# Attention rows stored as two half-precision planes and turned by transposing loads, with the stages of an output tile further apart

## The chip, the cores and the metric

The kernel runs on one core of one Trainium2 chip. A core has a matrix engine (TensorE, PE in the profile; its weight loads are listed apart as PEld), a vector engine (VectorE, DVE), an activation engine (ScalarE, ACT), a general engine (GpSimd, POOL) and an engine that mainly issues transfers (SyncE, SP). Each engine works through its own queue in the order in which the program fills it, and waits for the others through semaphores. Sixteen DMA engines move data between the chip's memory (DRAM), and the on-chip buffer (SBUF). PE writes its results to banks of a second on-chip memory (PSUM).

The metric is the device time of one execution in microseconds (us), as the median of several runs.

## What is computed

One decoder layer over 2048 positions of width 1024. The input `x` is normalised, scaled and shifted, and one projection makes everything that the two attention branches need. Branch A has 8 heads of width 64 with full causal attention and a forget-gate bias. Branch B has 8 query heads over 2 key/value heads, rotary positions, a window of 128 and a sink per head. Each branch output is multiplied by a SiLU gate; the two are joined and go through one output projection, a second normalisation and a gated residual sum.

```
h  = rms_norm(x, g_pre) * (1 + scale) + shift
qa, ka, va, fa, za, qb, kb, vb, zb = split(h @ w_in)
oa = forgetting_attention(qa, ka, va, fa + b_fgate) * silu(za)
ob = sliding_window_sink_attention(rope(qb), rope(kb), vb, sinks) * silu(zb)
y  = concat([oa, ob]) @ w_out
x + gate * rms_norm(y, g_post)
```

All inputs and the output are float32. The kernel keeps float32 accuracy on a half-precision matrix engine by writing each operand as a high plane (the value rounded to float16) and a low plane (the rest, in float16), and by summing three products: high by high, high by low, low by high.

## The kernel before

A program order is written out by hand. A list `late` holds work that is due some ticks later: `after(n, f)` runs `f` at the n-th following `tick()` (lines 185 to 195). Whatever `f` issues is then placed in the engines' queues at that point. Four stages follow each other.

1. Prologue (to about 166 us): the modulation, normalisation and turning of `x` into `hT`, and the first projections.
2. Windowed attention (about 166 to 396 us): 32 windows, one per pair of heads and pair of 128-row blocks (class `Pair`, lines 849 to 941, loop at lines 1122 to 1143). A window has four ticks. After the first tick come `maxima` (four DVE operations of line 881, and the sink columns copied by POOL at line 879); then units of projection work are filled in on PE; after the second tick `pv` of the window two earlier (PE, line 930); after the third tick `exps` (ACT, line 892) and `split`; the fourth tick issues the high split (ACT, line 909) with a transposing transfer from SBUF to SBUF on SP (line 910), and the next window's first tick the low split (DVE, line 914) with a second one (line 915). `scores` of the next window (PE, line 867) close the window. The output of `pv` is scaled one tick after it, in `out_` (line 934): DVE multiplies it by the reciprocal sums into `on` (line 936, [128 x 256] float32), and POOL issues its store to `o_d` (line 938).
3. Full attention (about 400 to 985 us): 8 heads of 20 steps (class `Step`, lines 1312 to 1368, loop from line 1613). A step is `exp32` (ACT, line 1335), a tick, `low` of the step before (DVE, line 1346), half of the filled-in work, `high` (ACT, line 1343), the next `scores` (PE, lines 1330 and 1331), a tick, `pv` of the step two before (PE, lines 1356 to 1359), and the other half. The filled-in work is projections (`punits`) and row maxima (`munits`: PE line 1281, DVE lines 1284 and 1286). At the end of each 512-row block of a head, 32 times in all, `pv` scales its result into `on` (DVE, line 1365) and SP issues the store to `o_d` (line 1366). In the last head the weights of the output projection are loaded and split, and the first output tiles begin: `load_o` and `load_z` at steps 1 to 6, `turn(4)` of tiles 0 and 1 at steps 6 and 8, products from step 10 on.
4. Output (about 985 us to the end): 16 tiles of 128 rows (class `Out`, lines 1440 to 1558). For tile t, `load` fetches the gate factors `z` and the 128 rows of `o_d` (SP, lines 1461 and 1455). `turn(lag)` issues eight PE transposes of float32 [128 x 128] blocks into two PSUM banks (line 1467), one tick later the gating by DVE (line 1476, two halves), two ticks later the sum of squares by ACT (line 1479), `lag` ticks later a small PE product over the partitions and a scale (line 1483), then the high split (ACT, line 1489) and the low split (DVE, line 1490). `product(n, k)` is one unit of three matmuls of 512 columns (line 1503); a tile has two halves n of eight units k. One tick after a half is done, `evac` has ACT sum its squares (line 1511) and DVE multiply it by the gate factors (line 1519), and gives its bank back. `root` and `store` follow 4 and 7 ticks after the second half (lines 1539 and 1553). A tick comes every second unit.

The order of stage 4 is the list `ounits` (lines 1562 to 1570): the products of tiles 0 and 1 first in alternation, then tile after tile, with `turn` of tile t+1 behind the third unit of tile t, and the load of tile t+2 ahead of tile t. `ofill` (line 1574) takes the next units; in the last head's steps it takes the first 33.

Buffers concerned: `onp` (line 700) has two `on`; `opa` (line 1171) and `opo` (line 1398) have two each of `ona` and, in `opa`, of the gate tiles `tz`. The row buffer of a tile is a part of `Ts[0]`, in rotation over t % 2 (lines 1454 and 1460).

Of the kernel before, what the change touches and what calls it, by code (L numbers as in the profile page):

```python
# [10 lines left out]
F32 = mybir.dt.float32  # L11
# [7 lines left out]
P = 128  # L19
# [21 lines left out]
def hybrid_layer(  # L41
# [33 lines left out]
    o_d = [dram.tile([CH, D], F32, name=f"o_d{t}") for t in range(NCH)]  # L75
# [112 lines left out]
    def after(n, f):  # L188
        late.append([n, f])
# [510 lines left out]
    onp = swa_pool("onp", 2)  # L700
# [148 lines left out]
    class Pair:  # L849
# [73 lines left out]
        def pv(self):  # L923
# [10 lines left out]
            def out_():  # L934
                on = onp.tile([P, 2, P], F32, tag="on", name="on")
                V.tensor_tensor(on[:].rearrange("p e (h d) -> p (e h) d", h=2), po[:],
                                self.rinv[:].unsqueeze(2).broadcast_to([P, 4, 64]), op=ALU.mult)
                G.dma_start(o_d[i // 4][(i % 4) * P:(i % 4 + 2) * P, (4 + j) * P:(5 + j) * P]
                            .rearrange("(e p) c -> p e c", p=P), on[:])
# [231 lines left out]
    op_ = foxl.enter_context(tc.tile_pool(name="opa", bufs=2, reuse_waits="tile"))  # L1171
# [140 lines left out]
    class Step:  # L1312
# [35 lines left out]
        def pv(self):  # L1348
# [12 lines left out]
            if self.last:  # L1361
# [4 lines left out]
                SP.dma_start(o_d[self.ci][:, hd * 64:(hd + 1) * 64].rearrange("(u p) d -> p u d", p=P), on[:])  # L1366
# [26 lines left out]
    def open_out():  # L1393
# [4 lines left out]
        op_ = foxo.enter_context(tc.tile_pool(name="opo", bufs=2, reuse_waits="tile"))  # L1398
# [16 lines left out]
        oio["r"] = [spare[:, 2 * CH * n:2 * CH * (n + 1)].bitcast(F32) for n in range(6)]  # L1415
        oio["j"] = [spare[:, CH * a:CH * b].bitcast(BF16) for a, b in ((12, 14), (14, 15), (15, 16))]
# [23 lines left out]
    class Out:  # L1440


        def __init__(self, t):
            self.t = t
            self.last = t == NB - 1
            self.cuts = (0, CH, CH + 3 * P, D) if self.last else (0, CH, D)
# [5 lines left out]
        def load_o(self):  # L1452
            t = self.t
            self.o = Ts[0][:, t % 2, :].bitcast(F32)
            SP.dma_start(self.o, o_d[t // 4][(t % 4) * P:(t % 4 + 1) * P, :])
# [7 lines left out]
        def turn(self, lag):  # L1463

            px = [bk[bank()][:].rearrange("p (k n) -> p k n", k=4) for _ in range(2)]
            for k in range(KT):
                PE.transpose(px[k // 4][:, k % 4, :], self.o[:, k * P:(k + 1) * P], ident[:])  # L1467
# [4 lines left out]

            def gate():
                for h in range(2):
                    z = self.z[:, 4 * h:4 * h + 4, :]
                    V.tensor_tensor(z, px[h], z, op=ALU.mult)  # L1476
# [9 lines left out]
            after(1, gate)  # L1486
            after(2, squares_)
            after(lag, scale_)
            after(lag + 1, lambda: A.activation(hi, self.z, AF.Copy, scale=self.sc[:]))  # L1489
            after(lag + 2, lambda: V.scalar_tensor_tensor(lo, self.z, self.sc[:], hi, op0=ALU.mult, op1=ALU.subtract))  # L1490

        def product(self, n, k):
# [15 lines left out]
            def evac():  # L1508
                if n == 0:
                    self.y = oio["y"]()  # L1510
                A.activation(oio["j"][1 + n % 2][:, :cc.stop - cc.start], py, AF.Square, accum_out=self.ss[:, n:n + 1])
                if self.last:
# [49 lines left out]
    ounits, oloads = [], {}  # L1562
    for t, n in [(0, 0), (1, 0), (0, 1), (1, 1)] + [(t, n) for t in range(2, NB) for n in range(len(outs[t].cuts) - 1)]:
        if n == 0 and t + 2 < NB:
            oloads[len(ounits)] = t + 2
        for q in range(KT):
            ounits.append(lambda t=t, n=n, q=q: outs[t].product(n, q))
            nxt = 2 if (t, n) == (0, 1) else t + 1 if n == 0 and 2 <= t < NB - 1 else None
            if q == 2 and nxt:
                ounits.append(lambda nxt=nxt: outs[nxt].turn(4))  # L1570
    opos = [0]
    N_IN = 4 * KT + 1

    def ofill(n, each=None):
        for _ in range(n):
            if opos[0] in oloads:
                outs[oloads[opos[0]]].load()
            ounits[opos[0]]()
# [151 lines left out]
```

## Time and profile before

| | |
|---|---|
| median of 3 runs (lowest to highest) | 1155.76 us (1154.94 to 1155.79) |
| the profiled execution: its own time | 1155.56 us |
| the profiled execution: span from first to last instruction | 1153.9 us |
| mean granted clock of TensorE | 0.995 |
| busy: PE, DVE, ACT, POOL | 1113.2, 909.9, 679.0, 166.4 us |
| DMA: moved in all, mean rate | 136.36 MB, 118 GB/s |

The span leaves out 1.66 us of the profiled execution's own time. Times in the views are microseconds from the start of the span; mean durations of single instructions are nanoseconds. A busy share is an average over stages with different limits. The chain of waits is followed back from the last instruction to whatever released each step. In a timeline row the bracket at the end tells how long the engine had sat idle and what ended that. In the rows by windows, the columns are the stretch, its length, the busy time of PE, PEld, DVE, ACT and POOL with their instruction counts, the granted clock, the mean busy share of the DMA engines, and GB/s. Matmuls are pipelined and their ends are modelled, so that a PE that shows as busy can hide gaps below about 0.15 us.

### The profile page before, as it was taken

To read this page: it belongs to the slowest core of one execution; us is meant where nothing else is said; L and a number is where in the kernel's file an instruction comes from. 1 tells how busy PE (TensorE), PEld (TensorE's weight loads), DVE (VectorE), ACT (ScalarE), POOL (GpSimd) and SP (SyncE) were. 2 spreads that over 40 slices of the span, in tenths; PEclk is the share of its full clock that TensorE was granted. 3 is DMA by queue.
4 is the path that set the end of the run, shared out by engine and by line. 5 is a ranking of instruction groups with operands and counts; after the bars stand their busy time and mean duration, and the time that the engine had idled before them with its cause. 6 is when DMAs were issued, how large, how long until landed. Compare 5 with 4: busy or idle time off the path is not lost. (4 is left out here: it accounts for less than half of the span.)

```text
span 1153.9 us, 27043 instructions
## 1 busy us (share of the span) xinstructions
PE 1113.2 (96%) x10514; PEld 651.5 (56%) x10514; DVE 909.9 (79%) x2330; ACT 679.0 (59%) x1124; POOL 166.4 (14%) x302
## 2 busy tenths in 40 slices
PE   5899999999999999999999999999999989999997
PEld 1466657655579865555555555555555555455554
DVE  6776668879888477889888989878797886766666
ACT  4666446556666515766767667676776698233331
POOL 2011122234322101111111201101010010000000
PEclk9999999999999999999999999999999999999999
DMA  9646426587777423323233232313121264464642
GB/s 330 223 138 169 107 71 135 111 171 141 174 145 121 96 61 84 85 78 81 78 82 98 61 89 63 66 38 98 43 56 38 66 185 154 156 211 166 203 168 88
DMA packets 162452, 136.36 MB, mean 118 GB/s; under 512 B 95356, under 2 KB 139428, under 8 KB 162324
## 3 DMA queue, kind: packets, MB, share of 16 engines
q1 hardware_dynamic: 152388, 106.39, 35.3%
q0 software_dynamic: 9456, 27.72, 9.1%
q8 instruction: 82, 1.34, 0.5%
q10 hardware_dynamic: 480, 0.53, 0.2%
q14 instruction: 46, 0.38, 0.1%
HBM read 70.97 MB, written 25.18 MB: 83 GB/s over the span
## 5 line engine op out<-in xcount | busy, mean ns | idle before, releaser
L1335 ACT ACTIVATE p<-sta,lift,scl_qk 128x1024 f32<-128x1024 f32 (+2 forms) x160 | 172.0, 1075 | 94.6 <-PE sta L1331 88.7
L335 PE MATMUL bk<-hT,wh_qk 128*128 128x512 f16 x768 | 197.9, 378 | 0.6 <-DVE a_m L1284 0.6
L1503 PE MATMUL bk<-wohl,oz 128*128 128x512 f16 (+2 forms) x792 | 172.5, 372 | 2.2 <-DVE oz L1490 1.0
L1346 DVE TENSOR_TENSOR pha<-p,pha 128x1024 f16<-128x1024 f32 (+2 forms) x160 | 169.7, 1061 | 0.0
L1343 ACT ACTIVATE pha<-p 128x1024 f16<-128x1024 f32 (+2 forms) x160 | 148.1, 926 | 31.6 <-POOL p L1339 26.3
L1284 DVE TENSOR_REDUCE a_m<-bk 128x1 f32<-128x512 f32 x192 | 129.3, 683 | 36.3 <-PE bk L1281 35.4
L1503 PEld LDWEIGHTS <-oz 128*128 128x128 f16 x792 | 75.8, 99 | 83.2 <-issue 1.8
L1356 PE MATMUL poa<-vt,pha 128*128 128x65 f16 x1088 | 116.5, 193 | 1.6 <-DVE ona L1365 1.6
L1359 PE MATMUL poa<-vt,pha 128*128 128x65 f16 x1088 | 116.0, 192 | 1.3 <-DVE pha L1346 1.3
L1358 PE MATMUL poa<-vt,pha 128*128 128x64 f16 x1088 | 116.3, 194 | 0.0
L1330 PE MATMUL sta<-T 128*128 128x512 f16 (+1 forms) x320 | 109.6, 347 | 4.5 <-ACT p L1335 4.5
L1281 PE MATMUL bk<-T 66*128 66x512 f16 (+2 forms) x320 | 110.5, 348 | 2.2 <-DVE a_m L1284 2.2
L1356 PEld LDWEIGHTS <-pha 128*128 128x128 f16 x1088 | 101.6, 97 | 16.3 <-DVE ona L1365 2.9
L335 PEld LDWEIGHTS <-wh_qk 128*128 128x128 f16 x768 | 70.2, 97 | 71.6 <-issue 2.9
L1358 PEld LDWEIGHTS <-pha 128*128 128x128 f16 x1088 | 101.0, 97 | 13.4
L1331 PE MATMUL sta<-T 69*128 69x512 f16 (+1 forms) x320 | 108.0, 348 | 0.0
L1359 PEld LDWEIGHTS <-pha 128*128 128x128 f16 x1088 | 100.8, 99 | 1.6 <-DVE pha L1346 1.6
L335 PE MATMUL bk<-hT,wh_za 128*128 128x512 f16 x384 | 99.8, 378 | 0.0
L353 PE MATMUL bk<-wh_va,hT 128*128 128x128 f16 x1536 | 92.6, 219 | 0.0
L1339 POOL TENSOR_SCALAR_AFFINE_SELECT p<-p 128x256 f32<-128x256 f32 x64 | 31.9, 499 | 413.4 <-ACT p L1335 408.5
L335 PE MATMUL bk<-hT,wh_zb 128*128 128x512 f16 x384 | 90.8, 379 | 0.0
L353 PEld LDWEIGHTS <-hT 128*128 128x128 f16 x1536 | 87.5, 98 | 5.9 <-issue 3.5
(497 smaller groups left out, 1851.5 us busy)
## 6 DMA issues: line engine op xcount, KB each, us to landing
hT<-in_x_dram SPq DMA_DIRECT2D x20, 512.0 KB
wa<-in_w_ada_dram SPq DMA_DIRECT2D x16, 512.0 KB
T<-stq SPq DMA_DIRECT2D x128, 64.0 KB
T<-z_d SPq DMA_DIRECT2D x16, 512.0 KB
T<-o_d SPq DMA_DIRECT2D x16, 512.0 KB
z_d<-tz POOLq DMA_DIRECT2D x30, 256.0 KB, 2.9
out_dram<-hT SPq DMA_DIRECT2D x15, 512.0 KB
xt<-in_x_dram SPq DMA_DIRECT2D x12, 512.0 KB
```

Source lines behind the costliest of these rows:

```text
L335: PE.matmul(ps, whl[:, a, k, :], hT[ci][:, b, k, :], start=(k == 0 and n == 0), stop=(k == KT - 1 and n == 2))
L353: PE.matmul(ps[:, u * P:(u + 1) * P], hT[ci][:, a, k, u * P:(u + 1) * P], whl[:, b, k, :], start=(k == 0 and n == 0), stop=(k == KT - 1 an ...
L1281: PE.matmul(mx[:, :w], T[0:XM, 0, i * P:(i + 1) * P], T[0:XM, 2, pc * CH:pc * CH + w], start=True, stop=True)
L1284: V.tensor_reduce(m3[:, u, pc:pc + 1], mx[:, :w], axis=AX.X, op=ALU.max)
L1330: PE.matmul(self.st[:, o:o + w], T[:, 3, kb_], T[:, 1, qc], start=True, stop=False)
L1335: A.activation(self.p32[:, :self.w], self.st[:, :self.w], AF.Exp, scale=scl[f"qk{self.hd}"][:], bias=lift[:])
L1343: A.activation(self.ph[:, 0, :self.w], self.p32[:, :self.w], AF.Copy)
L1346: V.tensor_tensor(self.ph[:, 1, :self.w], self.p32[:, :self.w], self.ph[:, 0, :self.w], op=ALU.subtract)
L1356: PE.matmul(po[:, u, :], ph[:, 0, pq], vt[:, b, hd, 0:65], start=(self.first and n == 0 and u == 0), stop=False)
L1358: PE.matmul(po[:, u, 0:64], ph[:, 0, pq], vt[:, b, hd, 65:VW], start=False, stop=False)
L1359: PE.matmul(po[:, u, :], ph[:, 1, pq], vt[:, b, hd, 0:65], start=False, stop=(self.last and n == len(self.blocks) - 1))
L1503: PE.matmul(py, self.hl[:, i, k, :], w_slot(8 * j + k)[:, cc], start=(k == 0 and m_ == 0), stop=(k == KT - 1 and m_ == 2))
```

## The change

- `o_d` is stored as two float16 planes [2, 512, 1024] in place of one float32 [512, 1024]: as many bytes, in rows half as long.
- Where an attention output is made (both `Pair.out_` and `Step.pv`), `on` is split: one tick later ACT copies it to the high plane `oh[:, 0]`, and two ticks later DVE subtracts to get the low plane `oh[:, 1]`, and the two planes are stored by two transfers in place of one (POOL in the windowed stage, SP in the full one). The buffers `onp`, `opa` and `opo` go from two to one of each tile.
- `load_o` becomes two transposing transfers from DRAM, one per plane, so that the rows of a tile arrive turned. `turn` issues no PE transposes and takes no PSUM banks; a DVE operation `join` adds the planes to float32 in the new tile `osum`, and the gating then is one DVE operation over [128 x 1024] from SBUF in place of two from PSUM.
- From tile 2 on `turn(7)` replaces `turn(4)`, gating and squares each come a tick later, and loads and turns have hand-written places: from tile 5 on the load is issued 36 units, and the turn 26 units, ahead of the tile's first product (tiles 2 to 4 are given by hand: loads at units 0, 8 and 30, turns at units 10, 22 and 39). An assertion at build time holds that the buffers' earlier users have been placed before.
- The DVE operation of `evac`, and with it the release of the bank, comes a tick after ACT's sum of squares (not in the last tile).

```diff
-    o_d = [dram.tile([CH, D], F32, name=f"o_d{t}") for t in range(NCH)]
+    o_d = [dram.tile([2, CH, D], F16, name=f"o_d{t}") for t in range(NCH)]
...
-    onp = swa_pool("onp", 2)
+    onp = swa_pool("onp", 1)
...
-                G.dma_start(o_d[i // 4][(i % 4) * P:(i % 4 + 2) * P, (4 + j) * P:(5 + j) * P]
-                            .rearrange("(e p) c -> p e c", p=P), on[:])
+                oh = onp.tile([P, 2, 2, P], F16, tag="oh", name="oh")
+
+                def low():
+                    V.tensor_tensor(oh[:, 1], on[:], oh[:, 0], op=ALU.subtract)
+                    for a in range(2):
+                        G.dma_start(o_d[i // 4][a, (i % 4) * P:(i % 4 + 2) * P, (4 + j) * P:(5 + j) * P]
+                                    .rearrange("(e p) c -> p e c", p=P), oh[:, a])
+
+                after(1, lambda: A.activation(oh[:, 0], on[:], AF.Copy))
+                after(2, low)
...
-                SP.dma_start(o_d[self.ci][:, hd * 64:(hd + 1) * 64].rearrange("(u p) d -> p u d", p=P), on[:])
+                oh = op_.tile([P, 2, 4, 64], F16, tag="oha", name="oha")
+
+                def put():
+                    V.tensor_tensor(oh[:, 1], on[:], oh[:, 0], op=ALU.subtract)
+                    for a in range(2):
+                        SP.dma_start(o_d[self.ci][a, :, hd * 64:(hd + 1) * 64].rearrange("(u p) d -> p u d", p=P),
+                                     oh[:, a])
+
+                after(1, lambda: A.activation(oh[:, 0], on[:], AF.Copy))
+                after(2, put)
...
+        oio["c"] = wpq.tile([P, D], F32, tag="whl", name="osum")[:].rearrange("p (k n) -> p k n", k=KT)
...
-            self.o = Ts[0][:, t % 2, :].bitcast(F32)
-            SP.dma_start(self.o, o_d[t // 4][(t % 4) * P:(t % 4 + 1) * P, :])
+            self.o = Ts[0][:, t % 2, :].rearrange("p (a k n) -> p a k n", a=2, k=KT)
+            for a in range(2):
+                SP.dma_start_transpose(self.o[:, a], o_d[t // 4][a, (t % 4) * P:(t % 4 + 1) * P, :])
...
-            px = [bk[bank()][:].rearrange("p (k n) -> p k n", k=4) for _ in range(2)]
-            for k in range(KT):
-                PE.transpose(px[k // 4][:, k % 4, :], self.o[:, k * P:(k + 1) * P], ident[:])
...
+            def join():
+                V.tensor_tensor(c, self.o[:, 0], self.o[:, 1], op=ALU.add)
+
             def gate():
-                for h in range(2):
-                    z = self.z[:, 4 * h:4 * h + 4, :]
-                    V.tensor_tensor(z, px[h], z, op=ALU.mult)
+                V.tensor_tensor(self.z, c, self.z, op=ALU.mult)
...
-            after(1, gate)
-            after(2, squares_)
+            after(1, join)
+            after(2 if lag > 4 else 1, gate)
+            after(3 if lag > 4 else 2, squares_)
...
                 if self.last:
+                    gated()
+                else:
+                    after(1, gated)
...
+    N_IN = 4 * KT
+    oloads = {0: 2, 8: 3, 30: 4}
+    oturns = {10: 2, 22: 3, 39: 4}
+    for t in range(5, NB):
+        oloads[2 * KT * (t - 3) + 12] = t
+        oturns[2 * KT * (t - 2) + 6] = t
...
+            if opos[0] in oturns:
+                outs[oturns[opos[0]]].turn(7)
```

33 lines of the change are left out of this document (18 added, 15 removed).

## The prediction, made before the changed kernel had run

> **What bounds the kernel now.** First the page, then the chain of waits, then each stage by windows and its timeline.
>
> ```profile
> span 1153.9 us, 27043 instructions
> PE 1113.2 (96%) x10514; PEld 651.5 (56%) x10514; DVE 909.9 (79%) x2330; ACT 679.0 (59%) x1124; POOL 166.4 (14%) x302
> ```
> PE is busy nearly throughout, so a change pays where it shortens PE's own queue, and costs where it makes PE wait. The chain that ended last shows the output stage:
>
> ```profile
> 1001.40 0.87 PE bk L1467 x8
> ...
> 1058.25 0.87 PE bk L1467 x8
> 1059.12 3.88 PE bk L1503 x18
> 1063.01 0.12 PE bk L1483 x2
> 1063.12 6.50 PE bk L1503 x30
> 1069.62 0.87 PE bk L1467 x8
> ...
> 1126.47 0.87 PE bk L1467 x8
> ```
> From 1001.40 us on there is nothing in it but PE, one instruction behind the other: a tile takes 1069.62 - 1058.25 = 11.37 us, of which the eight turns of line 1467 are 0.87 and the products 10.38. There are 12 such groups. The other engines have room in a tile, as its own window shows; the same view gives the seams of the stages:
>
> ```profile
> 1066.00:1077.37 11.37, 11.37 (x59) 5.83 (x58) 7.62 (x24) 3.68 (x7) 0.00 (x0) 1.00 0.55 184
> 166.00:383.00 217.00, 216.77 (x2710) 145.84 (x2708) 188.05 (x567) 131.53 (x337) 66.52 (x132) 1.00 0.72 140
> 250.00:280.00 30.00, 29.84 (x262) 15.11 (x261) 28.90 (x88) 21.57 (x56) 11.23 (x23) 1.00 0.81 161
> 500.00:940.00 440.00, 433.35 (x4377) 244.57 (x4376) 382.18 (x843) 307.67 (x402) 56.58 (x101) 1.00 0.29 74
> 940.00:950.00 10.00, 7.77 (x106) 5.32 (x105) 8.85 (x14) 10.00 (x14) 0.80 (x2) 1.00 0.38 108
> 965.00:970.00 5.00, 5.00 (x49) 3.20 (x48) 3.85 (x5) 4.82 (x9) 0.00 (x0) 1.00 0.39 152
> 985.00:990.00 5.00, 3.80 (x45) 2.67 (x46) 4.38 (x11) 0.52 (x2) 0.00 (x0) 1.00 0.14 31
> 990.00:995.00 5.00, 4.58 (x24) 2.07 (x23) 4.22 (x15) 1.68 (x4) 0.00 (x0) 1.00 0.98 307
> ```
> In an output tile DVE is busy 7.62 us and the DMA engines 0.55 x 11.37 = 6.3. In the windowed stage (second row) PE has no gap to speak of, but DVE is at 87%, and from 250 to 280 us at 96%: this is the stage with two engines at the limit. In full attention PE is busy 98% and DVE 87%. PE idles at two seams: from 940 to 950, where ACT has 10.00 of 10, and from 985 to 995, 1.6 us in all.
>
> **The change, part by part.** *Turns off PE.* The 12 groups in the closing chain give 12 x 0.87 = 10.4 us. Tiles 0 to 3 have a group each ahead of that. Tile 2's lies at 968.6, where PE is busy 5.00 of 5: another 0.9. Those of tiles 0 and 1 fall near 940 to 950, where ACT sets the pace: nothing. Tile 3's lies in the seam from 985, where PE waited for its gating and squares behind a full DVE queue; the change turns tile 3 some 14 units earlier, and what is late next is the last attention steps' own DVE work. Of the 1.6 us I take 1.0 (bounds 0 and 1.6).
>
> *The transposing loads.* No output tile has such a load yet; the windowed stage has transposes of the same shape, from SBUF. Here are its last one, the stretch of the last two, one of plain traffic alone, and one in which a tile's rows of 4 KB move:
>
> ```profile
> 382.80 1.88 SPq L915 DMA_TRANSPOSE ptb<-sp  x1
> 382.00:388.00 6.00, 6.00 (x123) 6.00 (x121) 2.93 (x12) 1.63 (x2) 1.22 (x3) 1.00 0.98 199
> 391.00:395.00 4.00, 4.00 (x85) 4.00 (x83) 0.00 (x0) 0.36 (x1) 0.00 (x0) 1.00 0.51 137
> 1071.50:1072.00 0.50, 0.50 (x4) 0.20 (x3) 0.46 (x3) 0.50 (x1) 0.00 (x0) 1.00 1.01 410
> ```
> The 6 us hold 0.98 x 6 = 5.9 us of all DMA engines and 1.19 MB: two transposes of 0.26 MB and 0.67 MB of plain traffic. The next row moves 0.55 MB in 2.0 us, so that plain part took 2.5 and a transpose (5.9 - 2.5) / 2 = 1.7 us. A tile loses its float32 row load (0.52 MB at 410 GB/s, 1.3 us) and gains two transposes: 6.3 - 1.3 + 3.4 = 8.4 us in a tile of 11.37 - 0.87 = 10.5. SP is held 1.9 us by the issue shown, twice in a tile, with the next row loads and stores queued behind: 3.8 of 10.5 us. The load stands 10 to 12 units (of 0.65 us) ahead of `join`, 6.5 to 7.8 us; a transpose issued at 382.80 had landed by 388, after 5.2. So I cost the loads at nothing; the cover is the slack of 2.1 us per tile, and a price follows as a rival.
>
> *DVE in an output tile.* `join` is a subtraction's equal (line 914 below, 1.23 us for 1024 columns), and gating in one piece is no dearer than in two. 7.62 + 1.2 = 8.8 us of 10.5, and the later tick of `evac` spares DVE a wait for ACT: nothing on the path. The bank held a tick longer is one of five, two of which `turn` no longer takes.
>
> *The split in the windowed stage.* Each of 32 windows gains an ACT copy, a DVE subtraction (both 256 columns) and a second POOL issue:
>
> ```profile
> L1184 ACT ACTIVATE wsq<-wsq 128x256 f32<-128x256 f32 x29 | 11.6, 402 | 0.0
> L938 POOL DMA_DIRECT2D o_d<-on x30 | 22.1, 736 | 90.1 <-DVE on L936 76.1 <-DVE kap_va L164 5.6 <-DVE sp L914 4.3
> ```
> Where do they stand? DVE's maxima of a window release ACT's exponentials, these the high split, this the low split on DVE, and behind that, in DVE's queue, come the next window's maxima: a ring through two in-order queues. The copy stands ahead of the high split in ACT's queue, and waits for `on`; the subtraction stands ahead of the low split. A cheap window and a dear one:
>
> ```profile
> 245.24 0.42 DVE L936 TENSOR_TENSOR on<-pob,b_ri 128x256 f32<-128x256 f32 x1
> 247.04 1.23 DVE L914 TENSOR_TENSOR sp<-sm__3372,sp 128x1024 f16<-128x1024 f32 x1 [1.38 <-ACT sp L909]
> 248.85 0.54 DVE L881 CUSTOM_DVE_ANT_0 sm__3471<-pss,bmask,snk 128x256 f32<-128x256 f32 x1
> 253.16 0.42 DVE L936 TENSOR_TENSOR on<-pob,b_ri 128x256 f32<-128x256 f32 x1
> 253.49 1.23 DVE L914 TENSOR_TENSOR sp<-sm__3471,sp 128x1024 f16<-128x1024 f32 x1
> 255.30 0.54 DVE L881 CUSTOM_DVE_ANT_0 sm__3574<-pss,bmask,snk 128x256 f32<-128x256 f32 x1
> ```
> ```profile
> 245.95 1.06 ACT L909 ACTIVATE sp<-sm__3372 128x1024 f16<-128x1024 f32 x1
> 252.18 0.19 ACT L892 ACTIVATION_READ_ACCUMULATOR sm__3471<-sm__3471,b_nb 128x1 f32 x1
> 252.40 1.06 ACT L909 ACTIVATE sp<-sm__3471 128x1024 f16<-128x1024 f32 x1
> ```
> ```profile
> 250.57 0.83 PE L867 MATMUL pss<-kst,stb 64*128 64x256 f16 x12
> 253.93 0.86 PE L930 MATMUL pob<-vb,ptb 128*128 128x64 f16 x24
> 257.32 0.83 PE L867 MATMUL pss<-kst,stb 64*128 64x256 f16 x12
> ```
> The ring took 255.30 - 248.85 = 6.45 us here, PE 257.32 - 250.57 = 6.75. In the first window `on` ends at 245.66, ahead of the split at 245.95: the copy delays the split and the low split by its own step, 0.3 (an operation of 0.42 follows another after 0.33, as 253.16 and 253.49 show), and the subtraction lies in the wait of 1.38. In the second, `on` ends at 253.58, 1.2 after ACT had finished the exponentials: the copy starts then, the split at 253.9, the low split at 255.0 in place of 253.49: 1.5. I walked through 31 windows so; in 16 the copy waits for `on`. The additions come to 21 us, from the first low split to the last:
>
> ```profile
> 180.84 1.23 DVE L914 TENSOR_TENSOR sp<-sm__2237,sp 128x1024 f16<-128x1024 f32 x1 [0.72 <-ACT sp L909]
> 381.18 1.21 DVE L914 TENSOR_TENSOR sp<-sm__5898,sp 128x1024 f16<-128x1024 f32 x1
> ```
> ```profile
>   PE pss L867: 6.2, 9
> SPq L1366 <- DVE ona L1365: 107.3, 18, 24.9
> ```
> The first of these rows is DVE waiting for PE's scores ahead of its maxima: 6.2 us that absorb as much. So PE pays between 0 and 21 - 6 = 15 us. Between these ends decides how far DVE may fall behind: the next `pv` needs `on` to be out of its bank. In the dear window `on` ended at 253.58 and PE's next `pv` began at 253.93, 0.35 later; in most others it was 2 to 5 us. Up to 248.85 the additions are some 8 us, less 2.3 of the waits; PE would be held there by 5, by 1 more in the next window, and later windows, with room again, hold it by 0 to 2. I take 7. POOL's two issues of 0.74 us come behind the rope product and ahead of the sink columns, which the exponentials need; they run beside the DVE part of the ring, and I count them in the 7. The single `oh` is free once its stores have landed, within a window.
>
> *The split in full attention.* 28 copies and subtractions lie in steps where PE is busy 98% and DVE 87%: 28 x 0.42 = 12 us more make DVE 90%. Most lies in DVE's waits for PE; from 0 to 3 us, I take 1. The second row above is SP waiting 107 us for `on` already, with row loads of the next head behind it; two ticks more of that are covered by the same idle. In the last head, ACT has no room from 940 to 950, and one copy falls there: 0.4.
>
> *Sum:* -10.4 - 0.9 - 1.0 + 7 + 1 + 0.4 = -3.9 us. The profiled execution took 1155.56 us, 1.66 more than its span and 0.2 under the median: 1151.7 us. Its own range, with the bounds 2 and 12 for the windowed stage, is 1146 to 1157.
>
> **The rivals.** *First: the ring's additions are covered.* ACT is at 61% in the windowed stage (131.53 of 217.00 us); if DVE's queue gives where I let it hold, the split costs nothing in either attention stage. Then 1155.6 - 12.3 = 1143.3 us. Against it: the 0.35 us above.
>
> *Second, on the other side: the ring takes PE's place as the bound of the windowed stage.* Then all that DVE's waits don't absorb is paid, 15 us, and 3 in full attention: 1155.6 - 12.3 + 15 + 3 + 0.4 = 1161.7 us. It decides from 0.3 us per window on, the difference of 6.75 and 6.45; the additions average 21 / 31 = 0.7. Against it: that holds only where DVE lags from the start, and in nine windows it waited for PE.
>
> *Third: the transposing loads bound the output stage.* They read DRAM, and the rows show transposes from SBUF only. With x per transpose a tile's DMA takes 5.0 + 2x; it passes 10.5 at x = 2.75. At twice the price, 3.4, a tile takes 11.8, and 12 tiles lose 16 us: 1151.7 + 16 = 1167 us. For it: this stage's other transfers are at 0.55 already. Against: 1.7 is far from 2.75. The Trainium skill, "VectorE: DVE Perf Modes", sections "The three transpose paths" and "Rules for kernel authors", speaks against the change: turn 128 x 128 on TensorE if the result may go to PSUM, at 390 ns against 1309 ns by DMA. An estimate by that page: 16 blocks, 21 us of transfers per tile. The trace does not agree for a run of blocks: sixteen of them took 3.4 us.
>
> *Fourth: DVE's order bounds the output stage.* If `join` waits for late loads 1.7 us or more per tile, 8.8 becomes 10.5; at 2.7 each tile costs a microsecond more: 1151.7 + 12 = 1164 us.
>
> **How the numbers follow.** Forecast 0.45, rivals 0.22, 0.20, 0.08 and 0.05. A measurement of this kernel can tell about 0.2%, 2.3 us, from no change: faster is below 1153.4, slower above 1158.1. Of the forecast's 0.45, 0.36 lies below 1153.4 and 0.09 within. The second rival reaches down to 1155 with a smaller addition: 0.06 within, 0.14 above. The third gives 0.02 and 0.06, the fourth 0.05 above. Faster: 0.36 + 0.22 = 0.58; same 0.09 + 0.06 + 0.02 = 0.17; slower 0.14 + 0.06 + 0.05 = 0.25. The range goes from the first rival to the second: 1142 to 1162, leaving out the third and the fourth and little of the others.
>
> **What would show it.** Right: no group of turns in the closing chain, a tile of 10.5 us there with DMA near 0.8, and a windowed stage that ends 5 to 9 us later, with PE waiting for `on` or for the transposed planes between 225 and 265 us. If that stage ends as before, the first rival holds; if DVE no longer waits for scores anywhere in it and it ends 12 us or more later, the second. Tiles of more than 10.6 us with DVE's `join` waiting on a DMA show the third, or, with DMA well under 0.9, the fourth. The prediction is wrong at its root if the closing chain still holds something else than products in every tile.

## The result, and the profile after

The changed kernel takes 1187.62 us, the median of 6 runs (1186.56 to 1189.49), against 1155.33 us for the kernel before in the same comparison (6 runs, 1154.94 to 1155.79): a ratio of 1.0281, with a 95% interval from 1.0269 to 1.0293. The forecast was 1151.7 us, the range 1142 to 1162. The profiled execution of after took 1189.49 us, with a span of 1187.8 and a mean granted clock of 0.982 (before: 1153.9 and 0.995).

The page's first lines answer to those shown of before:

```profile
span 1187.8 us, 27023 instructions
PE 1116.6 (94%) x10386; PEld 641.9 (54%) x10386; DVE 950.5 (80%) x2394; ACT 692.6 (58%) x1188; POOL 192.5 (16%) x334
```
PE has 128 instructions fewer, the turns, and is nevertheless busy 3.4 us longer. Where the time went is told by four distances, taken from the timelines: to the first exponential of full attention (435.33 us before; after, the row below), to the first of the last head, to the last one, and to the end of the span.

```profile
459.28 1.10 ACT L1343 ACTIVATE p<-sta,lift,scl_qk 128x896 f32<-128x896 f32 x1 [0.15 <-PE sta L1339]
```

| stretch, us | before | after | difference | predicted |
|---|---|---|---|---|
| up to the first exponential of full attention | 435.33 | 459.28 | +24.0 | +7 |
| heads 0 to 6 | 479.70 | 481.58 | +1.9 | +1 |
| the last head | 65.45 | 75.29 | +9.8 | -0.5 |
| from its last exponential to the end | 173.42 | 171.65 | -1.8 | -11.4 |

The prediction's 0.9 for the turns of tile 2 (at 968.8 us before) lies in the last head, so it is counted there, beside the 0.4 for ACT's copy.

**Output stage.** The chain of waits (columns: start, duration, what) over one tile:

```profile
1074.87 1.24 DVE osum L1493
1076.16 1.11 issue
1077.27 0.68 DVE hT L1551
1077.95 1.20 DVE hT L1589
1079.17 0.34 SPq L1590
...
1079.61 0.39 SPq L1481
...
1080.05 2.61 SPq L1475
...
1082.71 3.52 DMA T<-o_d
1086.32 1.24 DVE osum L1493
```
PE is not in it. DVE joins the planes, gates, and makes the last product of the tile that was finished before, which is what that tile's store waits for (line 1589); only then can SP issue that store (line 1590), and behind it in SP's queue stand the next tile's loads (lines 1481 and 1475), whose landing releases the next join. That is a closed ring, and it takes 1086.32 - 1074.87 = 11.45 us, against 10.5 predicted and 11.37 before. The rows by windows and by waits say the same, the first for that tile, the second for 1030 to 1180 us:

```profile
1074.87:1086.32 11.45, 10.70 (x52) 4.83 (x50) 8.72 (x24) 3.56 (x7) 0.00 (x0) 1.00 0.70 186
```
```profile
DVE osum L1493 <- DMA T<-o_d: 25.6, 10, 3.8
```
The DMA engines have room (0.70), and so has DVE (8.72 of 11.45), which yet waits for the planes ten times.

**Windowed stage.** Its whole stretch by windows, before and after, then full attention's after, and the windowed stage's waits (columns: total, times, longest):

```profile
166.00:395.00 229.00, 228.77 (x2946) 157.84 (x2944) 192.32 (x580) 134.14 (x341) 68.34 (x134) 1.00 0.71 141
```
```profile
166.00:419.00 253.00, 235.58 (x2947) 160.45 (x2946) 206.96 (x612) 142.63 (x372) 90.28 (x162) 0.98 0.67 123
```
```profile
525.00:965.00 440.00, 430.19 (x4327) 241.57 (x4325) 386.00 (x865) 308.14 (x422) 55.61 (x101) 1.00 0.30 70
```
```profile
POOL o_d L943 <- ACT oh L946: 59.4, 17, 5.7
...
DVE oh L941 <- ACT oh L946: 22.6, 19, 3.7
...
ACT oh L946 <- DMA o_d<-oh: 12.0, 8, 3.0
```
DVE is busy 206.96 of 253 us, 82% after 84% before, and PE, which had no gap, idles 17 us. So over the stage no engine is full, and they wait for each other. (Full attention, the third row, looks as before: PE at 98%, DVE at 88%.) One dear window shows how, first in POOL's timeline, then in ACT's:

```profile
361.73 1.66 POOL L735 TENSOR_TENSOR qs<-qs,sinT 128x512 f32<-128x512 f32 x1 [4.95 <-DMA qs<-qf]
363.34 1.47 POOL L943 DMA_DIRECT2D o_d<-oh  x2
364.81 0.86 POOL L879 COPY sm__5131<-snk 128x2 f32<-128x2 f32 x2
371.41 1.45 POOL L943 DMA_DIRECT2D o_d<-oh  x2 [5.74 <-ACT oh L946]
373.46 0.30 POOL L879 COPY sm__5305<-snk 128x2 f32<-128x2 f32 x2 [0.60 <-DVE sp L914]
```
```profile
365.59 0.51 ACT L892 ACTIVATE sm__5131<-sm__5131,b_nb 128x257 f32<-128x257 f32 x1 [4.10 <-POOL sm__5131 L879]
...
370.70 0.42 ACT L946 ACTIVATE oh<-on 128x256 f16<-128x256 f32 x1 [3.03 <-DMA o_d<-oh]
371.02 1.04 ACT L909 ACTIVATE sp<-sm__5131 128x1024 f16<-128x1024 f32 x1
```
The two stores hold POOL until 364.81, 1.47 us, so the sink columns and with them ACT's exponentials come that much later; the rest of ACT's 4.10 us of idling went to the rope product ahead of them on POOL and to DVE's maxima. ACT's next copy must wait another 3.03 until those very stores have landed, since there is one `oh`; the high split stands behind it. POOL's next stores wait 5.74 for that copy, and the next sink columns behind them. It is a ring as well, through POOL, ACT and the landing of a transfer.

A window's lag costs twice, since PE's clock was lower after PE had idled. PE's timeline around the first large loss, and that stretch by windows:

```profile
228.79 0.86 PE L930 MATMUL pob<-vb,ptb 128*128 128x64 f16 x24 [2.26 <-DVE on L936]
...
230.78 0.59 PE L335 MATMUL bk<-hT,wh_qb 128*128 128x512 f16 x2
235.37 1.89 PE L335 MATMUL bk<-hT,wh_qb 128*128 128x512 f16 x4 [4.00 <-DVE wh_qb L279]
```
```profile
230.00:235.00 5.00, 1.37 (x7) 0.41 (x5) 4.89 (x14) 1.83 (x7) 2.92 (x5) 0.93 0.53 107
235.00:240.00 5.00, 4.63 (x20) 1.76 (x21) 3.96 (x10) 3.31 (x8) 0.02 (x1) 0.50 0.24 56
```
PE waited 4.00 us for a weight split that stands in DVE's late queue, and in the next 5 us the granted clock was 0.50. The scores of the window there start 7.3 us later than before (237.19 against 229.86), when up to then they had been late by 0.1; those of the next are 9.2 us late (245.64 against 236.43), over a third of the 24.0. Here DVE itself was full (4.89 of 5 us), but its lateness has to do with POOL and ACT too. A window earlier, on POOL, ACT and DVE:

```profile
215.88 1.47 POOL L943 DMA_DIRECT2D o_d<-oh  x2
217.35 0.31 POOL L879 COPY sm__2901<-snk 128x2 f32<-128x2 f32 x2
```
```profile
217.58 0.51 ACT L892 ACTIVATE sm__2901<-sm__2901,b_nb 128x257 f32<-128x257 f32 x1 [2.39 <-DVE on L936]
```
```profile
220.74 1.41 DVE L279 SCALAR_TENSOR_TENSOR wh_zb<-wr_zb,w_sw,wh_zb 128x512 f16<-128x512 f32 x2 [3.15 <-ACT wh_zb L273]
```
ACT's row names DVE's `on`, but the exponentials don't read it. Of what they do read, DVE's maxima were done by 214.6, and the sink columns came last: they stood behind the two stores, 1.47 us. DVE then waited 3.15 us for ACT.

### The profile page after: what moved, and what is told of

Read it like the earlier page. It is cut to its first block, busy times and chain, and to the rows that moved or that the text cites. A ratio compares the mean times of both kernels' runs of the same rounds, so it can differ in the third digit from the quotient of the medians.

```text
span 1187.8 us, 27023 instructions
## 1 busy us (share of the span) xinstructions
PE 1116.6 (94%) x10386; PEld 641.9 (54%) x10386; DVE 950.5 (80%) x2394; ACT 692.6 (58%) x1188; POOL 192.5 (16%) x334
## 4 chain that ended last, share of the span: by engine, by line
PE 41%; DVE 19%; DMA 8%; issue 7%; ACT 6%; SPq 4%; POOL 2%; DVEq 0%; ACTq 0%; POOLq 0%
PE bk L335 17%; PE bk L1289 4%; PE sta L1338 4%; PE sta L1339 4%; DMA T<-o_d 4%; PE bk L1529 3%; DMA o_d<-oh 3%; DVE sp L914 2%; SPq L1475 2%; PE poa L1366 2%; PE poa L1367 2%; PE poa L1364 2%; ACT sp L909 2%; PE bk L353 2%; DVE osum L1493 1%
## 5 line engine op out<-in xcount | busy, mean ns | idle before, releaser
L1292 DVE TENSOR_REDUCE a_m<-bk 128x1 f32<-128x512 f32 x192 | 130.1, 684 | 33.9 <-PE bk L1289 32.9
L1364 PE MATMUL poa<-vt,pha 128*128 128x65 f16 x1088 | 118.0, 194 | 1.1 <-DVE ona L1373 1.1
L1367 PE MATMUL poa<-vt,pha 128*128 128x65 f16 x1088 | 117.5, 193 | 0.1
L1364 PEld LDWEIGHTS <-pha 128*128 128x128 f16 x1088 | 102.9, 98 | 15.6 <-DVE ona L1373 2.1
L1366 PEld LDWEIGHTS <-pha 128*128 128x128 f16 x1088 | 102.0, 98 | 13.5 <-issue 0.3
L1367 PEld LDWEIGHTS <-pha 128*128 128x128 f16 x1088 | 101.8, 99 | 0.2 <-DVE pha L1354 0.2
L335 PE MATMUL bk<-hT,wh_qb 128*128 128x512 f16 x384 | 91.5, 386 | 4.8 <-DVE wh_qb L279 4.8
```

The costliest lines, as they stand in the source:

```text
L335: PE.matmul(ps, whl[:, a, k, :], hT[ci][:, b, k, :], start=(k == 0 and n == 0), stop=(k == KT - 1 and n == 2))
L1364: PE.matmul(po[:, u, :], ph[:, 0, pq], vt[:, b, hd, 0:65], start=(self.first and n == 0 and u == 0), stop=False)
L1366: PE.matmul(po[:, u, 0:64], ph[:, 0, pq], vt[:, b, hd, 65:VW], start=False, stop=False)
L1367: PE.matmul(po[:, u, :], ph[:, 1, pq], vt[:, b, hd, 0:65], start=False, stop=(self.last and n == len(self.blocks) - 1))
```

## The experiments

One measure serves for the windowed stage: how far behind the kernel before the first exponential of full attention starts (435.33 us there). The stage's ends named in the expectations (419.1 us for the changed kernel, 395.1 for the one before) are the same thing, 40.2 us earlier. Four kernels with the same windowed stage, the changed one and three of the runs, came out at 22.5 to 24.9 us behind: differences under 2.5 us in it say nothing. Runs 3 to 5, 7 to 10 and 13 to 15 were executed once each, and all stage times are from one execution. In the same way the last head took 73.0 to 75.3 us in the twelve kernels that have it as the change made it.

**1. The output stage's loads ahead of the store.**

```diff
-        oloads[2 * KT * (t - 3) + 12] = t
+        oloads[2 * KT * (t - 3) + 8] = t
```


> Only the place of the output stage's loads changes: tile t's z load and its two transposing loads are issued four product units earlier (eight units into tile t-3 instead of twelve), so ahead of the store of the tile before on SP's queue instead of right behind it. Theory 1 (a ring through SP's queue: store waits for VectorE, VectorE's join waits for the transposed planes, the planes wait behind the store): the ring is cut, the tile's pitch falls from 11.5-12.5 us to about 10.5 us, and the time from 1187.6 to 1176-1180 us; VectorE's waits for the planes (25.6 us in 980 to 1187) fall under 5 us. Theory 2 (the transposing loads themselves bound the stage, by their 4.1 us of issue on SP or their 5-6 us in flight): the pitch stays over 11.3 us and the time at 1185-1189 us.

Measured: 1173.89 us (4 runs), 1.0152 of before [1.0135, 1.0169]. SP's queue now has the loads first, and the chain holds only PE again:

```profile
1081.12 0.37 SPq L1481 DMA_DIRECT2D T<-z_d  x1
1081.59 3.33 SPq L1475 DMA_TRANSPOSE T<-o_d  x2
1084.97 0.57 SPq L1526 DMA_DIRECT2D hT<-in_x_dram  x1
1085.64 0.38 SPq L1590 DMA_DIRECT2D out_dram<-hT  x1
```
```profile
1066.11 0.12 PE bk L1503 x2
1066.22 10.38 PE bk L1529 x48
1076.61 0.12 PE bk L1503 x2
```
```profile
1060.00:1081.00 21.00, 21.00 (x102) 9.86 (x101) 17.46 (x47) 7.12 (x14) 0.00 (x0) 1.00 0.82 201
```
A tile takes 1076.61 - 1066.11 = 10.50 us, and from the last exponential to the end it is 159.1 us, 12.5 less than in the changed kernel and 14.3 less than before. (In the thirteen kernels with the late loads this stretch took 169.5 to 171.7 us, in the four with the early ones 159.1 to 160.7.) VectorE no longer waits for the planes at all. Theory 1 holds, with a time 2 us below its range, and theory 2 falls: the same two transposing loads, with the same bytes, are hidden once nothing that waits stands ahead of them. The DMA engines are at 0.82.

**2. Windowed stage: the stores a step later on GpSimd.**

```diff
                 def low():
                     V.tensor_tensor(oh[:, 1], on[:], oh[:, 0], op=ALU.subtract)
+
+                def put():
                     for a in range(2):
...
                 after(2, low)
+                after(3, put)
```


> In the windowed half alone, the two stores of a window's attention rows are issued one quarter of a window later, so behind the next window's sink copies on GpSimd instead of ahead of them; ScalarE's copy and VectorE's subtraction keep their places. Theory 1 (the stores wait at the head of GpSimd's queue for the split, and the sink copies, the exponentials and the transposing loads of the next window stand behind them): the windowed stage ends at 400-408 us instead of 419.1, and the time is 1169-1177 us. Theory 2 (the added operations of ScalarE and VectorE, or the single tile that must land before it is written again, cost the time wherever the stores stand): it ends at 415-423 us, the time at 1184-1191 us. Here the tile is freed later than before, so theory 2 with the landing would show ScalarE's waits for the stores above the present 12 us.

Measured: 1195.28 us, 1.0343 of before [1.0327, 1.0358]; the stage 32.9 us behind, so 9 worse. GpSimd's 59.4 us of waits for the copy fell to 8.7, but ACT's waits for the landing grew from 12.0 to:

```profile
ACT oh L948 <- DMA o_d<-oh: 33.2, 18, 4.5
```
Theory 1 fails as it was put; what theory 2 said of the landing came. With one tile, a store that goes out later frees the tile later.

**3. The same stores through SP.** `G.dma_start` becomes `SP.dma_start`, nothing else.

> The two stores of a window's attention rows go out through SP's queue instead of GpSimd's; nothing else changes. Theory 1 (GpSimd blocked at its head): GpSimd's 59 us of waits at these stores go, and the windowed stage ends at 400-410 us if SP has the room; if SP's transposing loads of the probabilities are then late behind the waiting stores, it ends at 410-419 us with PE waiting for those loads. Theory 2 (the operations or the landing): 415-423 us.

Measured: 1175.58 us (one execution), the stage 14.3 us behind instead of 24.0, at the far end of theory 1's first range. So GpSimd's queue is part of the price.

**4 and 5. The split left out, with one tile and with two.**

```diff
-                on = onp.tile([P, 2, P], F32, tag="on", name="on")
-                V.tensor_tensor(on[:].rearrange("p e (h d) -> p (e h) d", h=2), po[:],
-                                self.rinv[:].unsqueeze(2).broadcast_to([P, 4, 64]), op=ALU.mult)
                 oh = onp.tile([P, 2, 2, P], F16, tag="oh", name="oh")
+                V.tensor_tensor(oh[:, 0].rearrange("p e (h d) -> p (e h) d", h=2), po[:],
+                                self.rinv[:].unsqueeze(2).broadcast_to([P, 4, 64]), op=ALU.mult)
```
The second run also sets `onp = swa_pool("onp", 2)`.

> The windowed half's split is left out: VectorE's multiply writes the high plane at once, and that plane is stored twice, so the low plane of the windowed heads is not computed. ScalarE's 31 copies and VectorE's 31 subtractions go; both stores stay on GpSimd where they stood. Theory 1 (what costs is the wait of the stores for a split that is two steps on): the stores wait for VectorE's multiply alone as before the change, and the windowed stage ends at 396-403 us. Theory 3 (what costs is the second store of each window: 31 more issues of 0.72 us on GpSimd, and 256-byte rows): it ends at 408-419 us.

> As the run without the windowed half's split (VectorE's multiply writes the high plane, which is stored twice; the low plane of the windowed heads isn't computed), but with two tiles for the planes in turn, so that a window's multiply doesn't wait until the last window's stores have landed. That run ended the windowed stage at 406 us with VectorE waiting 24.1 us for the landing of the stores. Theory L (the single tile's landing): those waits go and the stage ends at 397-401 us, 2 to 6 us behind the kernel before. Theory I (the second store's issue on GpSimd and its small rows): the stage still ends at 403-407 us.

Measured: 11.3 us behind (1174.05 us) with one tile, and 4.6 (1166.64 us) with two. The first lies between what theories 1 and 3 said, and its trace named a third cause, VectorE waiting for the tile's own stores:

```profile
DVE oh L936 <- DMA o_d<-oh: 24.1, 13, 3.8
```
With two tiles that wait is gone and theory L's range is met: 6.8 us are the tile's alone.

**6, 9 and 10. Who splits, and into how many tiles.** In runs 6 and 10 VectorE makes the whole split at once, in 6 with two tiles, in 10 with one; run 9 keeps the change's hand-over and gives it two.

```diff
+                V.tensor_tensor(hi, po[:], self.rinv[:].unsqueeze(2).broadcast_to([P, 4, 64]), op=ALU.mult)
+                for n in range(4):
+                    V.scalar_tensor_tensor(lo[:, n], po[:, n, :], self.rinv[:, n:n + 1], hi[:, n],
+                                           op0=ALU.mult, op1=ALU.subtract)
...
```


> The windowed half's split is made whole, but on VectorE alone and in one step: a multiply from PSUM writes the high plane, four small scalar_tensor_tensor from PSUM write the low one, both stores follow at once on GpSimd as before the change, and two tiles take turns. ScalarE's 31 copies and the f32 tile go. Theory H (the dear part is the hand-over VectorE to ScalarE to VectorE with a quarter of a window between, and the single tile): the stage ends at 398-406 us instead of 419.1, the time is 1168-1176 us. Theory W (the added work on VectorE costs wherever it stands; here it is some 0.2 us for each small operation, about 25 us in all): it ends at 412-420 us, the time 1181-1189 us.

> The windowed half's split as the change makes it (VectorE's multiply, ScalarE's copy a quarter of a window later, VectorE's subtraction and both stores another quarter later), but with two tiles for the planes in turn; the room comes from two small tiles of the gates and of the full half that share memory. Theory L (the single tile that must land before ScalarE may write it again is the main part): ScalarE's waits for the landing (12 us) and what follows them go, and the windowed stage ends at 403-410 us instead of 419.1. Theory H (the hand-over over two queues is the main part: GpSimd waits 59 us and VectorE 23 us for ScalarE's copy): it ends at 412-419 us.

> The split whole on VectorE as in the earlier run that ended the windowed stage 4.2 us behind the kernel before, but with one tile for the planes instead of two. Theory L: VectorE waits at each window until the last window's stores have landed (24 us of such waits where the split was left out with one tile), and the stage ends at 406-412 us, 10 to 16 us behind. Theory H (one tile is enough once the hand-over is gone): it ends at 400-403 us.

Measured, us behind before: hand-over with one tile (the change) 24.0, with two 15.7 (1179.06 us); VectorE alone with one 8.0 (1170.55 us), with two 4.2 (1168.06 us, 1.0107 of before [1.0090, 1.0124]). The groups of run 6 (columns: count, busy us in all with overlaps counted once, mean ns of one, idle before) show that VectorE is given *more* to do:

```profile
L939 DVE SCALAR_TENSOR_TENSOR oh<-pob,b_ri,oh 128x64 f16<-128x64 f32 x128 | 27.4, 276 | 1.1
...
L937 DVE TENSOR_TENSOR oh<-pob,b_ri 128x256 f16<-128x256 f32 x32 | 13.3, 416 | 3.3 <-PE pob L930 3.3
```
That is 27.4 us, in place of 13.0 for the change's subtractions, on an engine which the prediction had named as the one to watch: VectorE is busy 218.9 us in the stage instead of 207.0. Yet the stage is 20 us shorter, 16 with the one tile kept: theory H of run 6 holds, theory W falls. The two causes share the price: one tile costs 8.2 us under the hand-over and 3.8 without, the hand-over 16.0 us with one tile and 11.5 with two. In runs 9 and 10 the result lies at the border of, or between, the two theories' ranges, because each had one cause in mind.

**13 and 14. The hand-over with two tiles, its stores elsewhere.** The edits of runs 2 and 3 on run 9.

> The hand-over over ScalarE with two tiles (the run that ended the windowed stage 15.7 us behind the kernel before, GpSimd waiting 50 us at the stores), and the stores another quarter of a window later, behind the next window's sink copies. Theory G (GpSimd's queue order is the hand-over's price: the sink copies stand behind the waiting stores): the stage ends 4-9 us behind before. Theory Q (ScalarE's copy and VectorE's subtraction at the heads of their own queues are the price): 12-17 us behind.

> The hand-over over ScalarE with two tiles, and the two stores of each window through SP's queue instead of GpSimd's. Theory G: the stage ends 4-9 us behind before. Theory Q: 12-17 us behind. With one tile the same move took 9.7 us off.

Measured: 8.2 us behind (1171.98 us) with the stores behind the sink columns, 11.3 (1174.41 us) through SP, against 15.7 in run 9. So the move that cost 9 us with one tile gains 7.5 with two, and theory G holds for it; through SP it lies between G and Q. In run 13 GpSimd's waits at the stores are down from 49.7 us in run 9 to:

```profile
POOL o_d L946 <- ACT oh L949: 10.4, 3, 3.5
```
So the queue order on GpSimd and the one tile are two faults, and with one tile the second hid the first: the later stores that cured the order held the tile longer. Run 13 has neither fault and keeps the hand-over; its 8.2 us are what the hand-over itself is left with. In the first large loss, the scores that were 9.2 us late in the changed kernel (at 236.43 before) are 9.1 late in run 9, 4.9 in run 13 and 1.1 in run 6: there the second tile does nothing, and order and hand-over are the price.

**15. The rest.** As run 6, without the four small operations; the high plane is stored twice, at once.

> The low plane of the windowed heads is not computed: VectorE's multiply writes the high plane, and it is stored twice at once on GpSimd, with two tiles in turn. Beside the split on VectorE (4.2 us behind before) only the 128 small operations, 27 us of VectorE, are gone. Theory W (they are the rest of the price): the stage ends 0-2 us behind before. Theory R (two stores in half rows are): 3-5 us behind.

Measured: 0.5 us behind (1162.95 us): theory W. Two stores in half rows, at once and from two tiles, cost nothing that these runs can tell; run 5, which differs from it by sending the stores two ticks later, was 4.6 behind.

**7 and 8. The last head.** Run 7 alternates two `tz` tiles; run 8 puts `load_o` at steps 5 and 7, `turn(4)` at 7 and 9, products from step 11 on.

> Only the tile of the projections' gate values in the full-attention half (tz) is doubled again, as it was before the change. Theory Z (the first loads of w_out take over tz's memory and wait 10.7 us on SP for its store to land): the last head's first step to last step falls from 75.3 us by 2.5 to 3.5 us, and so does the time, to 1184-1185 us. Theory N (the wait is covered, and the last head is late by its own split, joins and loads): within 1 us of 1187.6.

> In the last head alone, the transposing loads of the first two tiles, their joins, and the first products stand one step later. At present the loads stand right behind the last head's stores of the same rows and SP waits for their landing, and VectorE's join waits 3.2 us for the planes. Theory E (the loads come too early for their data, and engines wait at their heads): the last head gets shorter by 2 to 5 us from 75.3, the time 1183-1186 us. Theory N (the added work of splits and joins is what is late): no gain, or 1 to 3 us longer since the products have a step less to lie in.

Measured, each once: 1185.01 us with a last head of 72.6 us, and 1184.07 with 71.7 (the time's other gain is in the windowed stage, within its spread). In the changed kernel the longest of SP's waits here was the one that run 7 should remove; the others are VectorE's for the planes and PE's for ACT:

```profile
SPq L1450 <- DMA z_d<-tz: 10.7, 1, 10.7
```
```profile
DVE osum L1493 <- DMA T<-o_d: 3.2, 1, 3.2
```
```profile
PE sta L1338 <- ACT p L1343: 6.9, 3, 4.0
```
In run 7 the same wait is there, 10.7 us in two pieces, and 72.6 is only 0.4 under the shortest of the unchanged last heads: theory Z isn't shown. In run 8 VectorE's wait for the planes is gone, and 71.7 is 1.3 to 3.6 under: some of theory E. Together, in runs 11, 12 and 16, the two edits gave 68.6 us three times, clearly less.

**11, 12 and 16. The edits together.** Run 11 has those of runs 1, 6, 7 and 8. Run 12 also lays the planes out as `[4, 2, 128, 1024]`, so that one transfer stores both. Run 16 has run 11's edits with the split as three operations of VectorE over the whole window.

> Four edits of the earlier runs on the changed kernel together: loads of the output stage eight units into a tile, the windowed split on VectorE with two tiles, two tz tiles, and the last head's rows a step later. If they add up: 1187.6 - 13.7 - 19.6 - 2.6 - 3.5 = 1148.2 us, 7 us (0.6%) under the kernel before; the windowed stage ends some 4 us behind it, the last head takes 69-70 us, a tile 10.5 us. If the last two edits overlap with the others (the same wait paid once): 1149-1153 us. Slower than before (over 1158) if the edits only move waits.

> As the four edits together, and the rows in memory laid out so that both planes of a window go out in one store of four rows of 128 columns instead of two stores (the full half's too). Theory I (the second store's issue on GpSimd, 31 times 0.73 us, is what leaves the windowed stage 4.2 us behind the kernel before): 2 to 4 us less than the four edits together, the windowed stage within 2 us of before. Theory W (the rest is VectorE's added 27 us of small operations): within 1.5 us of the four edits together.

> The four edits together (1152.0 us), with the windowed split on VectorE as three operations of the whole window (multiply to f32, copy to the high plane, subtraction to the low one) instead of one and four small ones: an estimated 0.42 + 0.2 + 0.33 us a window instead of 0.42 + 4 x 0.276 = 1.5 us, so some 17 us less of VectorE in the stage. Theory W (VectorE's time is the rest of the price): 1-3 us less, 1149-1151 us. Theory R (the stores): 1151.5-1152.5 us.

Measured: run 11 1151.99 us, 0.9971 of before [0.9958, 0.9983]; run 12 1152.05 us, 0.9977 [0.9967, 0.9987]; run 16 1150.65 us, 0.9959 [0.9945, 0.9972]. All three beat both kernels, by 0.2 to 0.4% against the one before and by 3% against the change. The windowed stage is 4.5, 4.3 and 4.7 us behind in them, the last head 68.6 us each, a tile 10.5 us. Run 11 is in the range for edits that overlap. In run 12 GpSimd is busy 22 us less in the stage (68.12 against 89.75 us) and nothing comes of it: theory I falls. Run 16 was to save 17 us of VectorE and saved little: its three operations take 0.42 + 0.30 + 0.43 = 1.14 us a window, but the four small ones, 0.276 us each, overlap and take 0.86 together, 1.27 with the multiply. VectorE is busy 217.0 us in the stage instead of 219.5, so run 16 can't test theory W: its time lies in that theory's range, its stage isn't shorter. The low plane's price (3.7 us between runs 6 and 15) may thus be VectorE's busy time, 218.9 us in run 6 and 194.2 in run 15, or the later start of the stores; the two were not tried apart. Run 16's smaller median, whose interval overlaps run 11's, is left unexplained.

## Why the prediction was wrong, point by point

The time came out 36 us over the forecast. By the table the windowed stage missed its term by 17.0 us, the last head by 10.3, the output stage by 9.6 and full attention by 0.9; the profiled execution is 1.9 us over the median.

**The turns off PE** (-10.4 in the chain, -12.3 in all) were sized rightly: with the loads in a place where nothing blocks them a tile takes 10.50 us for the 10.5 predicted, with DVE at 8.7 us a tile (8.8 predicted) and the DMA engines at 8.6 (8.4). The stretch to the end is 14.3 us shorter in run 1 and 12.8 in run 11, for 11.4; what is beyond is not explained. What failed is the step "so I cost the loads at nothing; the cover is the slack of 2.1 us per tile". It counted SP's time (3.8 us held, measured 4.1 and 3.3) and the landing, but only those transfers that come *behind* the loads. Just ahead of the load in SP's queue stands the store of a tile that was finished before, which waits for DVE behind the join: the prediction never walked SP's queue forward from the load's place. The fourth rival named the sign of this (join waiting on a transfer with the DMA engines well under 0.9) and, at 12 us, the price (12.5 here). DVE's order, to which it laid the loss, is half of the ring: the store's product stands behind the join. The other half, the loads behind that store, it didn't name, and it had a chance of 0.05.

**The third rival** is out: the transposing loads don't bound anything, at 0.82 of the DMA engines. What it cites of the Trainium skill, "VectorE: DVE Perf Modes", to turn on TensorE where PSUM will do, doesn't hold for this tile: with the loads placed well, run 1's is 10.50 us, and the one with PE's turns was 11.37.

**The windowed split** was given 7 us, with 15 as its upper bound; it cost 24.0. The failing step is the end of that part: the two issues on POOL "run beside the DVE part of the ring", and "the single `oh` is free once its stores have landed, within a window". Both sentences let a resource off without walking it. The walk over 31 windows followed DVE and ACT alone; the ring that decided ran through POOL's queue, where the stores stand ahead of the next window's sink columns, and through the landing of the stores. Without these two (run 13) the hand-over costs 8.2 us, which one execution can't tell from the 7 that the walk gave it; the two that were let off make the other 15.8. The bound of 15 was a bound of that walk, not of the change. The second rival asked for the right thing (the ring takes PE's place), and its sign came: DVE waits for scores nowhere in the changed kernel's stage. But it stopped at the same 15 us.

**The lower clock** was not in the sum at all. In the windowed stage PE is busy 235.58 us instead of 228.77 for the same products at a mean clock of 0.98: some 7 of the 24.0 us are slower matmuls, the other 17 are PE waiting.

**Full attention** was right: +1.9 for +1, within 0 to 3, and 1.9 to 2.0 in every run.

**The last head** was given 0.4 less 0.9 and cost 9.8. The prediction counted one copy by ACT and tile 2's turns, and looked at neither the loads that were to land in memory just released nor at row loads that stand right behind the stores of the same rows. The stretch by windows, before and after, and then two pieces of it after:

```profile
915.03:980.50 65.47, 61.12 (x651) 36.36 (x648) 50.71 (x86) 56.63 (x74) 5.20 (x10) 1.00 0.52 166
```
```profile
940.86:1016.15 75.29, 65.97 (x636) 37.41 (x633) 59.53 (x97) 59.07 (x80) 7.52 (x10) 0.89 0.67 154
```
```profile
970.00:975.00 5.00, 1.36 (x4) 0.52 (x4) 4.06 (x6) 3.65 (x7) 0.00 (x0) 0.66 0.69 172
975.00:985.00 10.00, 9.03 (x77) 5.81 (x76) 8.78 (x13) 8.38 (x11) 1.94 (x2) 0.50 0.44 114
```
PE is busy 4.9 us more, though the turns of three tiles are gone from the stretch, so about half of the loss is clock, and it falls behind a stretch in which PE was busy 1.36 of 5 us. Moving the rows and doubling `tz` took back 4.4 to 6.7 us (from 73.0 to 75.3 down to 68.6); the last 3.1 are open, and so is which of the two edits did how much.

## What to carry to other kernels

For each transfer that an edit moves, write down what stands ahead of it in its queue and what *that* waits for; a load behind a store, behind work that waits for the load before it, is a ring, whatever the DMA engines' share says. Here a buffer that a transfer read came free only when the transfer had landed (ACT waited up to 3.0 us for it), so halving the buffers put a DMA latency into an engine's queue; test such an edit together with the queue order, since here the single tile hid what a better order gains. And a hand-over to another engine to spare a busy one can cost more than the work: doing the split whole on the engine that held the data took 14 us more of that engine (221.0 us busy in run 10, 207.0 in the change, one tile in both) and made the stage 16 us shorter.

## What the runs showed of the hardware

The granted clock was 0.50 in the stretches right after PE had waited 4.00 us (windowed stage) and 4.03 us (last head). The Trainium skill, "TensorE: Matmul & The Clock Gate", section "What's actually happening", says that the clock is halved after an idle window of about 3.4 us and comes back after as long a busy one. On the drop the traces agree. The return took longer: some 5.7 us after PE began again at 235.37 in the windowed stage (an estimate from 0.50 up to 240 and the mean of 0.89 from 240 to 245), and over 11 in the last head, from 973.64 to past 985, where PE still had gaps of 1 us in 10.

Two transposing loads of [128 x 1024] float16 from DRAM held SP 3.3 to 4.1 us, and the join that needed them began 6.3 us after the first was issued (1080.05 to 1086.32). In the changed kernel the 64 KB stores of the windowed stage landed in 3.0 us at the median, 6.5 at most.
